# Head norm with its root on GpSimd and one VectorE step a head, and four changes of order, in a hybrid decoder step on one core

## The chip, the cores and the metric

The program runs on one core of one Trainium2 chip. A core has five engines, each with its own queue of instructions, which it works off in order: TensorE (PE in the profile; its weight loads are shown as PEld), VectorE (DVE), ScalarE (ACT), GpSimd (POOL) and SyncE (SP), which here only issues transfers. An instruction starts when the one ahead of it in its queue is done with issuing and the semaphores that it waits for have been raised. Data lies in SBUF, matmul results in the eight banks of PSUM, inputs and outputs in HBM. The metric is the time of one execution in device microseconds; a time quoted for a kernel is the median of several runs.

## What is computed

One inference step of a one-layer decoder on 544 tokens: a prompt of 512 tokens and 8 samples of 4 tokens each, D = 1024.

```python
proj = jnp.einsum('btd,de->bte', x, w_in) + b_in
q, k, v, g, ca, cg = jnp.split(proj, 6, axis=-1)
...
o, r_new = retention(q, k, v, r0, log_gamma)
ret_out = jax.nn.silu(g) * head_norm(o).reshape(b, t, RET_WIDTH)
conv_out, buf_new = conformer_conv(ca, cg, buf, dw_kernel, dw_bias, conv_ln_g, conv_ln_b)
mix = jnp.einsum('bte,ed->btd', jnp.concatenate([ret_out, conv_out], axis=-1), w_out)
x = layer_norm(ALPHA * x + mix, ln1_g, ln1_b)
ffn = peer(x.reshape(b * t, D_MODEL), w_query, sub_keys_1, sub_keys_2, peer_u, peer_v)
x = layer_norm(ALPHA * x + ffn.reshape(b, t, D_MODEL), ln2_g, ln2_b)
```

`head_norm` normalises each of the four heads' 128 outputs of a token: `(x - mean) * rsqrt(var + 1e-5)`. `peer` takes for each token and each of 8 heads the best 16 of 128 x 128 experts (the sum of two key scores), weighs each expert's output vector by a softmax gate times the gelu of the token's product with the expert's input vector, and adds them up.

## The kernel before

**Tokens and stages.** The first 128 prompt tokens, with the 32 sample tokens, go through projection, convolution, retention, output projection and norm first. Then come the other 384 prompt tokens, whose work shares the engines with the expert stage of the first 128. The experts are done in two ways. For the first 128 prompt tokens, the samples and the next 128 prompt tokens ("I", "Is" and "Ib" in the profile) GpSimd fetches each chosen expert's two vectors by an indirect transfer of 1 MB for 128 tokens (L587, line 587). VectorE takes the product (L590), ScalarE the gelu and the gate (L598, L599), and VectorE adds the weighted vector (L604). For the last 256 prompt tokens all experts are computed densely: for each of the 128 values of the first key ("rows" below) TensorE multiplies the 128 experts' input vectors with the tokens (`scores_of`, L815, weights from `ut`), ScalarE takes the gelu, the gates are spread into the same layout by a second kind of matmul (`build`: L893 to L906, multiplied in at L945, stored at L947 and L963), and TensorE multiplies the row's weights with its output vectors (`v_products`, L930, one load `v_row` of 512 KB each) into four PSUM banks, pB00 and pB01 for the first 128 of these tokens (b = 0), pB10 and pB11 for the others (b = 1).

**What sets the order.** The program is written in the order in which it is to be thought of. A scheduler with a model of durations then puts each engine's instructions into the order of their planned starts, the earlier written first where several are ready. `behind(a, b)` tells it to place `a` after `b`; it is a matter of order only and makes no semaphore. `hold` and `fence` use it to place gather products behind certain steps. Tiles come from pools that turn over a few buffers, so the next user of a buffer waits for the last reader of the one before: `mm` banks of PSUM (`mmps`; four in the key search), two score tiles in SBUF for `retrieve`, four buffers `uvp` for the rows, two PSUM tiles `sp` for a pair of rows' scores.

**Head norm** (`head_norm`, L317 to L336) is called five times: for chunk 0 of the prompt (L672), for the samples in `retain_s`, and for chunks 1 to 3 in `retain`. The retention output comes without the decay factor exp((i+1) log gamma) of its rows, so the norm multiplies the variance by the factor's square (`gq2`), adds epsilon and takes the root on GpSimd (`rsqrt`, L182 to L185), multiplies by the factor (`gq`), and makes a bias of minus mean times scale (L331, `hnb`); ScalarE then applies scale and bias to each head (L334, `on`). TensorE transposes the heads (`gate_heads`, L341) and VectorE multiplies them with the gates (L342).

**The other places.** Four loads of the samples' convolution cache `u_s` stand at L658 on GpSimd's queue, before the first gated projection. The chosen lists are turned into key sums for the build at L836 to L857, for g = 0 and 1: three transposes each (L848), behind the retrievals of all eight heads and ahead of those for "b" and "s" (`topk_of`, `retrieve` with scores L532, copies L535). While the first keys are built, `first_keys` multiplies the first eight rows for b = 0 alone (`AHEAD` = 8). `phases` then does b = 1 for rows 4 to 7, whose buffers still hold them, loads rows 0 to 3 a second time for b = 1, and goes on with row 8, both halves at once. The last four rows are loaded, and then written as all of b = 0 before all of b = 1; the two closing norms follow (L1021 on). The scheduler put these last sixteen products in the order of the rows, both halves of each in turn. `rope` (L201 on) copies a projected head to SBUF on ScalarE (L219), and TensorE then turns it (L209).

Of the kernel before, what the change touches and what calls it, by code (L numbers as in the profile page):

```python
# [24 lines left out]
CW, CK = 512, 31  # L25
# [19 lines left out]
def _consts():  # L45

    f = np.float32
    parts = {}
    pos = np.concatenate([np.arange(128), PAST + np.tile(np.arange(SQ), SB), np.arange(128, NP)]).astype(f)
    inv = (f(10000.0) ** (-np.arange(0, DH, 2, dtype=f) / f(DH))).astype(f)  # L50
    ang = (pos[None, :] * inv[:, None]).astype(f)
    cos, sin = np.cos(ang).astype(f), np.sin(ang).astype(f)
    parts["cos"] = np.concatenate([cos, cos], 0)
    parts["sin"] = np.concatenate([-sin, sin], 0)
    lg = np.log(1.0 - 2.0 ** (-5.0 - np.arange(H)))
    i = np.arange(C)
    mp = (i[:, None] <= i[None, :])[:, None, :] * (DH ** -0.5) * np.exp(-(i + 1.0)[:, None] * lg)[:, :, None]
    parts["mask_p"] = mp.reshape(128, -1)
    s = np.arange(NS)
    si, sb = s % SQ, s // SQ  # L60
    ms = ((sb[:, None] == sb[None, :]) & (si[:, None] <= si[None, :]))[:, None, :] * (DH ** -0.5)
    ms = ms * np.exp(-(si + 1.0)[:, None] * lg)[:, :, None]
    z = np.zeros((128, H * NS))
    z[:NS] = ms.reshape(NS, -1)
    parts["mask_s"] = z
    parts["kc_p"] = (DH ** -0.5) * np.exp((C - 1.0 - i)[:, None] * lg)
    parts["gq_p"] = np.exp((i + 1.0)[:, None] * lg)
    parts["gq2_p"] = np.exp(2 * (i + 1.0)[:, None] * lg)
    for n, v in (("kc_s", (DH ** -0.5) * np.exp((SQ - 1.0 - si)[:, None] * lg)),
                 ("gq_s", np.exp((si + 1.0)[:, None] * lg)), ("gq2_s", np.exp(2 * (si + 1.0)[:, None] * lg)),  # L70
                 ("blk", (sb[:, None] == np.arange(SB)[None, :]) * 1.0)):
# [23 lines left out]
def tile_step(ctx: ExitStack, tc: tile.TileContext, a, o):  # L95
# [222 lines left out]

    def head_norm(po, n, kind):

        st = small("hst", [128, H, 6])
        mv = small("hmv", [128, H, 2])
        for h in range(H):
            V.bn_stats(st[:n, h], po[:n, h * DH:(h + 1) * DH])
            V.bn_aggr(mv[:n, h], st[:n, h])
        rs = small("hrs", [128, H])
        V.tensor_mul(rs[:n], mv[:n, :, 1], cc("gq2_" + kind)[:n])
        rsqrt(rs[:n], rs[:n])
        V.tensor_mul(rs[:n], rs[:n], cc("gq_" + kind)[:n])
        nb = small("hnb", [128, H])  # L330
        steps[kind] = V.scalar_tensor_tensor(nb[:n], mv[:n, :, 0], -1.0, rs[:n], op0=OP.mult, op1=OP.mult)  # L331
        on = small("on", [128, 512])
        for h in range(H):
            S.activation(on[:n, h * DH:(h + 1) * DH], po[:n, h * DH:(h + 1) * DH], AF.Identity,  # L334
                         bias=nb[:n, h:h + 1], scale=rs[:n, h:h + 1])
        return on  # L336

    def gate_heads(on, n, gT, c0):
# [295 lines left out]
    for g, (w_, r_) in GSP.items():  # L634
# [19 lines left out]
    nc.sync.dma_start(cst[0], a["consts"])  # L654
    W0[2] = load_w(a["w_in"], 2 * 512, [t.rearrange("p (k e) -> p k e", k=8) for t in (
        gx.tile([128, 2 * D], F32, name="g"), per.tile([128, 8 * n], F32, name="x1T")[:, 0:2 * D])])
    for m in range(4):
        nc.gpsimd.dma_start(u_s[:, m, :, 0:CK - 1], a["cacheT"][m * 128:(m + 1) * 128])  # L658
    glu(W0[5], W0[4], xT0, 160, 0, 128)
    conv(y0, 128, 0)  # L660
    nc.scalar.dma_start(cst[1], a["consts2"])
    w = W0[2]
    v0 = project_v(w, xT0, 0, 128, lead2[:, 1280:1792])
    lastq = rope(load_win(0), 0, xT0, 160, 0, both(q0, qS))
    lastk = rope(load_win(1), 1, xT0, 160, 0, both(k0, kS))
    silu_gate(load_win(3), xT0, 160, both(g0, gS), True)
    normed = conv_norm(y0, 128)
# [135 lines left out]
    def place2(e):  # L803

        g = max(i for i in range(4) if E0S[i] <= e)
        return GW[g][:, e - E0S[g]:e - E0S[g] + 2]

    def scores_of(e, ne=1):

        sp = pdn.tile([128, 2, ND], F32, name="sp")  # L810
        for i in range(ne):
            u = uvp.tile([128, D], F32, name="uv").rearrange("p (k e) -> p k e", k=8)
            nc.sync.dma_start(u, a["ut"][e + i])
            for k in range(8):
                T.matmul(sp[:, i], u[:, k], x1T[:, k, NG2:], start=(k == 0), stop=(k == 7), skip_group_check=True)  # L815
        return sp[:, 0:ne] if ne > 1 else sp[:, 0]

    qs = rp.tile([128, 16, n], F32, name="qs")
# [14 lines left out]
            c0 = NG2 + 128 * g  # L833
            retrieve(lambda h, s: qs[:, h * 2 + s, c0:c0 + 128], [h0, h0 + 1], 128, 1, eg[:, g], eg[:, 2 + g], h0)
    wps.close()
    for g in range(2):  # L836
        ef = eg[:, g].rearrange("p h k -> p (h k)")
        ei = rp.tile([128, 128], I32, name="ei")
        V.tensor_copy(ei, ef)
        V.tensor_scalar(ei, ei, NK - 1, None, op0=OP.bitwise_and)  # L840
        e1 = rp.tile([128, 128], F32, name="e1")
        V.tensor_copy(e1, ei)
        e2 = rp.tile([128, 128], F32, name="e2")
        V.tensor_sub(e2, ef, e1)
        V.tensor_scalar(e2, e2, 1.0 / NK, None, op0=OP.mult)
        p = mmps().rearrange("p (q t) -> p q t", q=4)
        for q, t in enumerate((e1, e2, eg[:, 2 + g].rearrange("p h k -> p (h k)"))):
            T.transpose(p[:, q], t, ident)  # L848
        gr = rp.tile([128, 128], F32, name="e2")
        S.activation(gr, p[:, 2], AF.Copy)  # L850
        cs = slice(g * 128, (g + 1) * 128)
        S.activation(e1T[:, cs], p[:, 0], AF.Copy, scale=-1.0)
        S.activation(e2T[:, cs], p[:, 1], AF.Copy)
        for q in range(3):
            V.tensor_copy(gtT[:, q, cs], gr)
            if q < 2:
                V.tensor_sub(gr, gr, gtT[:, q, cs])  # L857
    topk_of("b", NS, range(0, PH, 2))
    topk_of("s", 0, range(2))
    for e in range(E0S[2], E0S[3], 2):  # L860
        S.activation(place2(e), scores_of(e, 2), AF.Gelu)
    gbs = ExitStack()
    gb = gbs.enter_context(tc.tile_pool(name="gb", bufs=1, side="right", reuse_waits="tile"))
    GW[0] = gb.tile([128, EG[0], ND], F32, name="Gb")
# [104 lines left out]
            v_products(e, vt, b)  # L969

    def phases():
        for e in [*range(AHEAD - UV, AHEAD), *range(AHEAD - UV)]:
            v_products(e, ahead[e] if e >= AHEAD - UV else v_row(e), 1)
            yield
        for e in range(len(ahead), EG[0]):
            v_stage(e)
            yield
        gbs.close()
        gd = ctx.enter_context(tc.tile_pool(name="gd", bufs=1, side="right", reuse_waits="tile"))
# [14 lines left out]
        ends = [(e, v_row(e)) for e in range(NK - UV, NK)]  # L994
        for b in range(2):
            for e, vt in ends:
                v_products(e, vt, b)
                yield

    def fetched():  # L1000
# [73 lines left out]
```

## Time and profile before

| | |
|---|---|
| timed runs, us | 1555.4, 1565.19, 1567.76; median 1565.19 |
| profiled execution, us | 1557.44, its span 1555.7 |
| mean granted TensorE clock over the span | 0.983 |
| VectorE, ScalarE, GpSimd busy, share of the span | 79%, 37%, 24% |
| bytes moved by transfers | 505.85 MB, mean 325 GB/s |
| share of the chain that ended last: PE, DVE, DMA, issue | 55%, 20%, 12%, 9% |

A line of a group or timeline names the source line, the engine and the operation, then the tile written and the tiles read, and the shapes. In a timeline the first number is the start in us from the beginning of the span and the second the duration, and a bracket at the end gives the engine's idle time before it and what ended that. Line numbers are those of the kernel before; in the changed kernel the same lines stand up to four lines earlier as far as the key search, and up to twelve later behind it.

### The profile page before, as it was taken

The numbers are of one execution on the slowest core, as the hardware profiler recorded it, in microseconds if no ns is written. First come the engines' busy times: TensorE is split into PE (matmuls) and PEld (weight loads), VectorE is DVE, ScalarE is ACT, GpSimd is POOL, SyncE is SP. The second block draws the span as 40 slices with busy tenths as digits, with TensorE's granted clock in tenths as the row PEclk, the third lists the DMA queues.
The fourth block names the chain that finished last, engine by engine and source line by source line (L and its number), as shares of the span: only waits on it lengthen the run. The fifth ranks groups of instructions, "written<-read, shape, count | busy, mean of one in ns | idle before, by whom it ended". The sixth has DMA issues, their size and how long they took to land.

```text
span 1555.7 us, 20736 instructions
## 1 busy us (share of the span) xinstructions
PE 1484.1 (95%) x7046; PEld 1004.1 (65%) x7046; DVE 1227.7 (79%) x3151; ACT 581.4 (37%) x1633; POOL 369.6 (24%) x329
## 2 busy tenths in 40 slices
PE   6999999897999999999999999999999999999997
PEld 6978667565866668788888884444566555543333
DVE  4779998978747999999978988666777777766664
ACT  2224453125112333333534898426992111111110
POOL 2001225322312222312231101222223222322210
PEclk9999999998999999999999999999999999999999
DMA  9648787985688779999999624999999999999993
GB/s 362 243 153 353 252 297 257 347 334 206 226 339 341 273 260 363 358 330 346 366 382 360 240 88 177 394 350 402 347 372 394 423 424 424 424 424 424 424 410 121
DMA packets 100119, 505.85 MB, mean 325 GB/s; under 512 B 10247, under 2 KB 21255, under 8 KB 57125
## 3 DMA queue, kind: packets, MB, share of 16 engines
q0 software_dynamic: 42240, 305.12, 50.4%
q1 hardware_dynamic: 51325, 192.05, 32.4%
q10 hardware_dynamic: 6448, 7.36, 1.5%
q8 instruction: 55, 0.90, 0.2%
q14 instruction: 51, 0.42, 0.1%
HBM read 499.12 MB, written 5.80 MB: 325 GB/s over the span
## 4 chain that ended last, share of the span: by engine, by line
PE 55%; DVE 20%; DMA 12%; issue 9%; POOL 3%; ACT 2%; DVEq 0%; SPq 0%; POOLq 0%; ACTq 0%
PE pB L930 27%; PE sp L815 11%; DMA g<-in_uv_dram,I 6%; PE mm L199 5%; PE mm L486 5%; DVE acc L604 4%; DVE g L590 4%; PE mm L906 3%; POOL g L587 2%; DMA g<-in_uv_dram,Is 2%; DMA g<-in_w_in_dram 2%; DMA uv<-in_uv_dram 1%; PE mm L310 1%; DVE B L901 1%; DVE score L516 1%
## 5 line engine op out<-in xcount | busy, mean ns | idle before, releaser
L815 PE MATMUL sp<-x1T,uv 128*128 128x256 f32 x2048 | 464.1, 383 | 5.2 <-DMA uv<-in_ut_dram 2.8
L604 DVE SCALAR_TENSOR_TENSOR acc<-g,wgt,acc 128x1024 f32<-128x1024 f32 x285 | 364.5, 1279 | 102.0 <-ACT wgt L599 100.4
L815 PEld LDWEIGHTS sp<-x1T,uv 128*128 128x128 f32 x2048 | 384.7, 191 | 78.5 <-issue 28.2
L598 ACT ACTIVATE act<-act 128x1 f32<-128x1 f32 x288 | 57.8, 201 | 625.7 <-DVE g L590 625.4
L587 POOL DMA_INDIRECT g<-in_uv_dram,I x128 | 166.9, 1304 | 460.1 <-DVE acc L604 259.2
L590 DVE SCALAR_TENSOR_TENSOR g<-g,x1g 128x1024 f32<-128x1024 f32 x160 | 195.2, 1222 | 71.8 <-DMA g<-in_uv_dram,Ib 50.5
L587 POOL DMA_INDIRECT g<-in_uv_dram,Ib x128 | 140.6, 1098 | 442.0 <-DVE acc L604 293.7
L199 PE MATMUL mm<-x1T,w 128*128 128x384 f32 (+1 forms) x512 | 178.3, 504 | 1.5 <-ACT score L535 1.2
L590 DVE SCALAR_TENSOR_TENSOR g<-g,x 128x1024 f32<-128x1024 f32 x128 | 154.8, 1214 | 31.0 <-DMA g<-in_uv_dram,I 30.9
L930 PE MATMUL pB<-uv,Ga 128*128 128x512 f32 x352 | 162.1, 604 | 0.2
L893 ACT ACTIVATE off<-row,e1T 128x128 bf16<-128x128 bf16 x512 | 158.0, 388 | 1.0
L199 PEld LDWEIGHTS mm<-x1T,w 128*128 128x128 f32 x512 | 97.4, 192 | 73.7 <-issue 40.3
L930 PE MATMUL pB<-uv,Gb 128*128 128x512 f32 x256 | 113.5, 597 | 4.9 <-DMA uv<-in_uv_dram 4.5
L930 PEld LDWEIGHTS pB<-uv,Ga 128*128 128x128 f32 x352 | 63.7, 189 | 83.4 <-issue 63.1
L930 PE MATMUL pB<-uv,Gd 128*128 128x512 f32 x256 | 115.5, 599 | 0.8
L930 PEld LDWEIGHTS pB<-uv,Gd 128*128 128x128 f32 x256 | 46.7, 190 | 69.7 <-issue 69.5
L930 PEld LDWEIGHTS pB<-uv,Gb 128*128 128x128 f32 x256 | 47.4, 190 | 60.7 <-issue 52.9
L906 PEld LDWEIGHTS <-A 128*128 128x128 bf16 x1536 | 60.5, 96 | 31.3 <-issue 21.3
L901 DVE TENSOR_TENSOR B<-M,gtT 128x768 bf16<-128x768 bf16 (+1 forms) x192 | 69.4, 416 | 9.4 <-PE mm L906 9.2
L930 PE MATMUL pB<-uv,Gc 128*128 128x512 f32 x160 | 72.8, 600 | 0.0
L895 ACT ACTIVATE A<-off 128x1024 bf16<-128x1024 bf16 x64 | 67.4, 1053 | 9.3 <-PE mm L906 8.5
L906 PE MATMUL mm<-B,A 128*128 128x96 bf16 (+1 forms) x1536 | 63.9, 191 | 7.3 <-DVE Gc L947 6.5
(274 smaller groups left out, 1675.4 us busy)
## 6 DMA issues: line engine op xcount, KB each, us to landing
uv<-in_uv_dram SPq DMA_DIRECT2D x132, 512.0 KB
uv<-in_ut_dram SPq DMA_DIRECT2D x128, 512.0 KB
w<-in_w_in_dram SPq DMA_DIRECT2D x18, 1024.0 KB
w<-in_w_query_dram SPq DMA_DIRECT2D x16, 1024.0 KB
w<-in_w_out_dram SPq DMA_DIRECT2D x7, 1024.0 KB
g<-in_uv_dram,I POOLq DMA_INDIRECT x128
keys<-in_state_retention_dram ACTq DMA_DIRECT2D x4, 512.0 KB
out_dram<-keys SPq DMA_DIRECT2D x4, 512.0 KB
```

Source lines behind the costliest of these rows:

```text
L199: T.matmul(p[:, :n], w[m // 2][:, k, (m % 2) * 128:(m % 2 + 1) * 128], xT[:, k, c0:c0 + n], start=(k == 0), stop=(k == 7))
L486: last = T.matmul(banks_[q][:n, s * 256:(s + 1) * 256], src[:, k, c0:c0 + n], wo[q * 2 + s][:, k0 + k, :], start=(xT is None and k0 == 4 a ...
L587: G.indirect_dma_start(out=t, out_offset=None, in_=a["uv"], in_offset=bass.IndirectOffsetOnAxis(ap=idx[:, k:k + 1], axis=0))
L590: dot = V.scalar_tensor_tensor(t[:, :D], t[:, :D], 1.0, x1, op0=OP.mult, op1=OP.mult, accum_out=act[:, 0:1])
L598: S.activation(act[:, 1:2], act[:, 0:1], AF.Gelu)
L604: V.scalar_tensor_tensor(acc, v, wgt, acc, op0=OP.mult, op1=OP.add)
L815: T.matmul(sp[:, i], u[:, k], x1T[:, k, NG2:], start=(k == 0), stop=(k == 7), skip_group_check=True)
L893: S.activation(off[:, t], row, AF.Abs, bias=e1T[:, t1 + t:t1 + t + 1])
L895: S.activation(A, off, AF.Relu, bias=1.0, scale=-1.0)
L901: V.tensor_tensor(B[:, q], M, pairs_of(gtT[:, q], t1).to_broadcast([128, TB // 2, ne, 2]), op=OP.mult)
L906: mm = T.matmul(pt[:, t % nt], A[:, t - t1], B[:, q, (t - t1) // 2, :, t % 2], start=(q == 0), stop=(q == 2))
L930: ps_.append(T.matmul(pB[b][q], W[:, b * 128:(b + 1) * 128], vt[:, q * 512:(q + 1) * 512], start=False, stop=(e == NK - 1), skip_group_che ...
```

## The change

Five edits. The head norm's decay factor moves into the constant: `ce` is epsilon divided by the factor's square, which is added to the variance, and the factor cancels, so `gq`, `gq2` and three small VectorE steps go. The add and the power run on GpSimd, and VectorE subtracts the mean and scales in one step a head, instead of ScalarE. The cache's four loads are written behind the first rotary projection, with `behind`. The key sums move into a function that is called after 34 of the 44 rows of a stretch have been written, and their transposes are placed behind the last matmul of the pair of rows just written. In `phases` the reloaded rows 0 to 3 alternate with rows 8 to 11. The last rows' b = 1 products are placed behind the last one of b = 0.

```diff
-    parts["gq_p"] = np.exp((i + 1.0)[:, None] * lg)
-    parts["gq2_p"] = np.exp(2 * (i + 1.0)[:, None] * lg)
+    parts["ce_p"] = EPS * np.exp(-2 * (i + 1.0)[:, None] * lg)
...
     def head_norm(po, n, kind):
...
         rs = small("hrs", [128, H])
-        V.tensor_mul(rs[:n], mv[:n, :, 1], cc("gq2_" + kind)[:n])
-        rsqrt(rs[:n], rs[:n])
-        V.tensor_mul(rs[:n], rs[:n], cc("gq_" + kind)[:n])
-        nb = small("hnb", [128, H])
-        steps[kind] = V.scalar_tensor_tensor(nb[:n], mv[:n, :, 0], -1.0, rs[:n], op0=OP.mult, op1=OP.mult)
+        G.tensor_add(rs[:n], mv[:n, :, 1], cc("ce_" + kind)[:n])
+        G.tensor_tensor(rs[:n], rs[:n], mhalf[:n].to_broadcast([n, H]), op=OP.pow)
         on = small("on", [128, 512])
         for h in range(H):
-            S.activation(on[:n, h * DH:(h + 1) * DH], po[:n, h * DH:(h + 1) * DH], AF.Identity,
-                         bias=nb[:n, h:h + 1], scale=rs[:n, h:h + 1])
+            steps[kind] = V.tensor_scalar(on[:n, h * DH:(h + 1) * DH], po[:n, h * DH:(h + 1) * DH], mv[:n, h, 0:1],
+                                          rs[:n, h:h + 1], op0=OP.subtract, op1=OP.mult)
...
-    for m in range(4):
-        nc.gpsimd.dma_start(u_s[:, m, :, 0:CK - 1], a["cacheT"][m * 128:(m + 1) * 128])
     glu(W0[5], W0[4], xT0, 160, 0, 128)
...
     lastq = rope(load_win(0), 0, xT0, 160, 0, both(q0, qS))
+    for m in range(4):
+        behind(nc.gpsimd.dma_start(u_s[:, m, :, 0:CK - 1], a["cacheT"][m * 128:(m + 1) * 128]), lastq)
...
             for k in range(8):
-                T.matmul(sp[:, i], u[:, k], x1T[:, k, NG2:], start=(k == 0), stop=(k == 7), skip_group_check=True)
+                latest[:] = [T.matmul(sp[:, i], u[:, k], x1T[:, k, NG2:], start=(k == 0), stop=(k == 7),
+                                      skip_group_check=True)]
...
-    for g in range(2):
+    def lists(g, mark):
...
         for q, t in enumerate((e1, e2, eg[:, 2 + g].rearrange("p h k -> p (h k)"))):
-            T.transpose(p[:, q], t, ident)
+            behind(T.transpose(p[:, q], t, ident), mark)
...
     for e in range(E0S[2], E0S[3], 2):
         S.activation(place2(e), scores_of(e, 2), AF.Gelu)
+        if e - E0S[2] == 32:
+            for g in range(2):
+                lists(g, latest[0])
...
     def phases():
-        for e in [*range(AHEAD - UV, AHEAD), *range(AHEAD - UV)]:
-            v_products(e, ahead[e] if e >= AHEAD - UV else v_row(e), 1)
+        for e in range(AHEAD - UV, AHEAD):
+            v_products(e, ahead[e], 1)
             yield
-        for e in range(len(ahead), EG[0]):
+        for e in range(AHEAD, EG[0]):
             v_stage(e)
+            if e < 2 * AHEAD - UV:
+                v_products(e - AHEAD, v_row(e - AHEAD), 1)
             yield
...
         for b in range(2):
             for e, vt in ends:
-                v_products(e, vt, b)
+                ps_ = v_products(e, vt, b)
+                if b:
+                    for p in ps_:
+                        behind(p, last)
+                else:
+                    last = ps_[-1]
                 yield
```

More of the change, by code (lines that the diff above doesn't have):

```diff
@@ L66, in _consts @@
     parts["kc_p"] = (DH ** -0.5) * np.exp((C - 1.0 - i)[:, None] * lg)
-    parts["gq_p"] = np.exp((i + 1.0)[:, None] * lg)
-    parts["gq2_p"] = np.exp(2 * (i + 1.0)[:, None] * lg)
+    parts["ce_p"] = EPS * np.exp(-2 * (i + 1.0)[:, None] * lg)
     for n, v in (("kc_s", (DH ** -0.5) * np.exp((SQ - 1.0 - si)[:, None] * lg)),
-                 ("gq_s", np.exp((si + 1.0)[:, None] * lg)), ("gq2_s", np.exp(2 * (si + 1.0)[:, None] * lg)),
+                 ("ce_s", EPS * np.exp(-2 * (si + 1.0)[:, None] * lg)),
                  ("blk", (sb[:, None] == np.arange(SB)[None, :]) * 1.0)):
@@ L806, in place2 @@
         return GW[g][:, e - E0S[g]:e - E0S[g] + 2]
+    latest = []
     def scores_of(e, ne=1):
```

## The prediction

> **What bounds the kernel now.** I read the page first, for which engine is full.
>
> ```profile
> span 1555.7 us, 20736 instructions
> ...
> PE 1484.1 (95%) x7046; PEld 1004.1 (65%) x7046; DVE 1227.7 (79%) x3151; ACT 581.4 (37%) x1633; POOL 369.6 (24%) x329
> ...
> L815 PE MATMUL sp<-x1T,uv 128*128 128x256 f32 x2048 | 464.1, 383 | 5.2 <-DMA uv<-in_ut_dram 2.8
> ```
>
> TensorE is busy in 1484.1 of 1555.7 us, idle in 71.6. The change removes no matmul, so it can gain only what TensorE waits for, what it loses at a lower clock, and the tail after its last matmul. One row of keys is 16 instructions of the L815 group, 16 x 464.1/2048 = 3.6 us; I use this unit below. The second view is the list of TensorE's waits (line waiting, what it waited for: us in total, times, longest).
>
> ```profile
> PE mm L341 <- ACT on L334: 9.6, 2, 6.6
> ...
> PE mm L906 <- DVE Gc L947: 6.5, 8, 1.7
> PE pB L930 <- DMA uv<-in_uv_dram: 4.5, 4, 1.8
> PE mm L209 <- ACT blk L219: 4.2, 1, 4.2
> PE mm L848 <- DVE e L842: 3.0, 1, 3.0
> ...
> PE mm L486 <- DVE g L342: 0.8, 1, 0.8
> ...
> PE mm L848 <- DVE e L845: 0.7, 1, 0.7
> ```
>
> Five of these belong to the change: the head norm (L341, 9.6, and its gate L342, 0.8), the key sums' transposes (L848, 3.7), the rows loaded again (L930, 4.5), and, through the order of ScalarE's queue, the rotary turn (L209, 4.2). The third view is the busy time by stretch: the first number is the stretch, then PE, PEld, DVE, ACT, POOL, and the granted clock, DMA share and GB/s last.
>
> ```profile
> 280.00:320.00 40.00, 35.76 (x105) 20.57 (x104) 39.87 (x62) 8.01 (x26) 14.55 (x12) 0.91 0.93 346
> 360.00:400.00 40.00, 31.70 (x154) 21.61 (x155) 31.39 (x63) 14.77 (x36) 15.79 (x15) 0.83 0.72 257
> 478.00:772.00 294.00, 284.56 (x1273) 226.16 (x1272) 286.43 (x1094) 99.30 (x240) 71.20 (x59) 0.99 0.89 327
> 836.00:958.00 122.00, 116.08 (x1060) 95.57 (x1057) 114.70 (x397) 109.04 (x312) 7.37 (x7) 0.99 0.50 178
> ```
>
> Two things stand here. Where TensorE waits long, its clock also falls: 0.83 over 360 to 400, against 1.00 or 0.99 in undisturbed stretches. And the key search (478 to 772) is full on both sides: TensorE 284.6, VectorE 286.4 of 294. A wait that goes there on one side may come back on the other.
>
> **Head norm.** For the prompt's chunks 2 and 3 the chain of events is this.
>
> ```profile
> 361.04 0.75 PE L341 MATMUL mm<-cst,on 128*128 128x128 f32 x4 [2.96 <-ACT on L334]
> 362.40 2.08 PE L357 MATMUL mm<-blk 128*128 128x128 f32 x8 [0.60 <-DVE Rst L381]
> 371.13 0.48 PE L341 MATMUL mm<-cst,on 128*128 128x128 f32 x1 [6.65 <-ACT on L334]
> ...
> 361.47 0.88 DVE L381 SCALAR_TENSOR_TENSOR Rst<-Rst,mm 128x128 f32<-128x128 f32 x4
> 362.26 0.37 DVE L325 BATCH_NORM_AGGREGATE hmv<-hst 128x2 f32<-128x6 f32 x4
> 363.10 0.62 DVE L253 SCALAR_TENSOR_TENSOR blk<-mm,cols,sg 128x384 f32<-128x384 f32 x1 [0.47 <-ACT sg L251]
> 363.63 1.28 DVE L604 SCALAR_TENSOR_TENSOR acc<-g,wgt,acc 128x1024 f32<-128x1024 f32 x1
> ...
> 364.90 0.68 DVE L359 TENSOR_TENSOR sc<-mm,cst 128x512 f32<-128x512 f32 x1
> ...
> 370.42 0.16 DVE L331 SCALAR_TENSOR_TENSOR hnb<-hmv,hrs 128x4 f32<-128x4 f32 x1
> ...
> 370.62 1.50 ACT L334 ACTIVATE on<-mm,hnb,hrs 128x128 f32<-128x128 f32 x4 [3.82 <-DVE hnb L331]
> ...
> 366.17 0.25 POOL L184 TENSOR_SCALAR hrs<-hrs 128x4 f32<-128x4 f32 x1
> 366.50 1.05 POOL L185 TENSOR_TENSOR hrs<-hrs,mhalf 128x4 f32<-128x4 f32 x1
> ```
>
> Before, a head norm is VectorE, GpSimd twice, VectorE twice (0.16 each), then four ScalarE steps (1.50). After, it is GpSimd's add and power, then four VectorE steps. The new step is not in this trace; its nearest row is the four L381 steps of the same 128x128 size, 0.88 us, and its upper end ScalarE's 1.50. The GpSimd add lies between the 0.25 of L184 and the 1.05 of L185; I take 0.25. VectorE so gains 20 x 0.22 = 4.4 us of work over five head norms and loses 15 small steps of 0.16 (2.4), on an engine that is not full here (31.4 of 40).
>
> In the changed program's queues (the built program's order, not a run) the four steps of the first chunk stand ahead of three gather products that L331 stood behind, so its transpose finds them done. For the second chunk they stand right after L359, and I walk VectorE's queue: L381 ends at 362.35 now, 0.9 later with the four new steps before it, 363.25; then the aggregates 0.37, two gather sums of 1.28 and two gate steps of 0.62, and L359's 0.68, in all 368.1; the first step ends at 368.3. TensorE takes its transpose there instead of at 371.13: **2.8 us**. It doesn't get the whole 9.6, because the score matmuls L357 between the two transposes wait for L381, which moves 0.9 us the other way: the 2.96 is mostly exchanged for a longer wait there. Bounds: 0 and 9.6. For chunk 1 the four steps start where L331 ended, so the 0.8 of L342 goes: **0.8 us**. GpSimd's queue puts the roots among the gathers at nearly the same places; behind a root wait only gathers whose buffers come free later anyway. The samples' norm hides under TensorE's conv and projections.
>
> The Trainium skill ("GPSIMD Engine Reference", section 4.1 Engine selection) advises against GpSimd for a two-input elementwise step, about twice as slow as VectorE. By that the add would cost about 2 x 0.16 = 0.3 instead of 0.25 and the sum would stay. No run here shows it yet.
>
> **The rotary turn.** This is an effect of queue order only.
>
> ```profile
> 290.87 0.20 ACT L598 ACTIVATE act<-act 128x1 f32<-128x1 f32 x1 [2.14 <-DVE g L590]
> ...
> 294.21 0.20 ACT L598 ACTIVATE act<-act 128x1 f32<-128x1 f32 x1 [2.81 <-DVE g L590]
> 294.45 0.30 ACT L599 ACTIVATE wgt<-act,GT 128x1 f32<-128x1 f32 x1
> 294.65 0.56 ACT L219 ACTIVATE blk<-mm,cols 128x384 f32<-128x384 f32 x1
> ...
> 295.26 1.65 PE L209 MATMUL mm<-blk,cst 128*128 128x384 f32 x2 [4.24 <-ACT blk L219]
> ```
>
> The copy L219 stands in ScalarE's queue behind a gather's activation, which waits for VectorE. In the changed order one pair of L598 and L599 fewer stands ahead of this copy. Behind the pair of 290.87 it would start 0.44 later, as it does now behind 294.21, and 0.9 later again for the four new VectorE steps: 292.2 instead of 294.65. So the wait shrinks by **2.4 us** (bounds 0 and 4.2).
>
> **Key sums' transposes.** They are put behind a matmul of row 33, and the scores of the next search (L532) move up in their place. The 3.7 us of L848 go. But what paces the stretch is VectorE, whose instructions before the first build step are the same but for one sum (L604). In the changed queue TensorE has 58 rows ahead of the first build product instead of 61, 3 x 3.6 = 10.8 us less to fill the time with. Those rows aren't lost: they come in the build, where TensorE waits 6.5 us for L947 and ScalarE is full 109 of 122. VectorE begins its search 12 L815 instructions (2.7 us) earlier and has up to 294 - 286.4 = 7.6 us of idle time to win. So the end of this stretch lies between 3.7 + 2.7 = 6.4 us of gain and 10.8 - 2.7 = 8.1 us of loss; I take **0**.
>
> **Late rows.** TensorE waits 4.5 us for four reloaded rows that need only half a row's matmuls each.
>
> ```profile
> 967.00 1.98 PE L930 MATMUL pB<-uv,Gb 128*128 128x512 f32 x4 [1.80 <-DMA uv<-in_uv_dram]
> ...
> 979.21 3.70 PE L930 MATMUL pB<-uv,Gb 128*128 128x512 f32 x8 [1.08 <-DMA uv<-in_uv_dram]
> ```
>
> Rows land about (979.21 - 967.00)/4 = 3.1 us apart. Half a row takes 1.8 us, so TensorE starves; a whole and a half row take 5.4 us for two loads, 2.7 each, so it starves less but later. The first 1.80 remains, since the first load comes no sooner. Of 2.7 I take **1.5 us** (bounds 0 and 2.7; SP's queue holds the same loads, in another order).
>
> **Last keys by halves.** The four banks end one after the other:
>
> ```profile
> 1489.36 57.03 PE L930 MATMUL pB<-uv,Gd 128*128 128x512 f32 x128
> ...
> 1543.85 0.70 DVE L452 BATCH_NORM_STATS2 lst<-pB 128x6 f32<-128x512 f32 x1 [18.17 <-PE pB L930]
> ...
> 1547.56 0.68 DVE L452 BATCH_NORM_STATS2 lst<-pB 128x6 f32<-128x512 f32 x1
> 1548.16 1.40 DVE L466 SCALAR_TENSOR_TENSOR g<-g,lrs,lnb 128x512 f32<-128x512 f32 x2
> ...
> 1551.22 1.41 DVE L466 SCALAR_TENSOR_TENSOR g<-g,lrs,lnb 128x512 f32<-128x512 f32 x2
> ```
>
> TensorE ends at 1546.39, but the last bank's statistics wait for the other half's norm until 1547.56, and its aggregate for that half's L466 until 1549.56. With one half done before the other's last eight matmuls, the first norm fits in VectorE's idle 18.17 us. The last bank then starts at about 1546.4, 1.1 us sooner, and the aggregate doesn't wait for L466 (1549.56 - 1547.56 - 0.68 = 1.3): **2.2 us** (bounds 1.1 and 2.4).
>
> **Cache loaded late: nothing.** In the changed program's GpSimd queue the four loads stand where they stood, after the memset and ahead of the norm's rows, with no wait. The order asked for binds only instructions of the same queue. I take 0.
>
> The sum is 2.8 + 0.8 + 2.4 + 0 + 1.5 + 2.2 = **9.7 us**. The profiled execution took 1557.44 us around its span of 1555.7; the three timed runs lie at 1555.4, 1565.19 and 1567.76, median 1565.19. The profiled one is 7.8 below the median, among the quick ones. I set the sum against the middle of both, 1561.3: 1551.6, or **1552 us**.
>
> The clock is not in the sum. At 0.83 over 40 us some 2 x 0.17 x 40 = 13.6 us ran at half speed, at 0.91 some 7.2; at most 6.8 and 3.6 us were lost. The Trainium skill ("TensorE: Matmul & The Clock Gate", section HAM oscillation) says that an idle gap of more than about 3.4 us halves the clock. The trace agrees in that the two stretches hold waits of 6.65 and 4.24. By that rule the turn's wait, cut to 1.8, would keep the full clock, and the sum would be up to 3.6 us larger; the head norm's new gap of some 4 us would still trip it.
>
> **Rivals.** (a) *The waits go entirely, and the clock with them.* 9.6 + 0.8 + 4.2 + 3.7 + 2.7 + 2.4 = 23.4 us, and up to 10.4 of clock: 1527 to 1538. For it speaks that the new steps depend on little; against it that L357 still waits for L381. Chance 0.20. (b) *The key search gives it back.* TensorE reaches the first build product before VectorE does and waits out its 8.1 us: 1561.3 - 9.7 + 8.1 = 1560. Chance 0.15. (c) *Slower: the search's scores stall TensorE in its queue.* L532 now stands among rows 8 to 30, each group needing a bank that a ScalarE copy frees, whose own target waits for a full VectorE; all L815 rows queue behind it. The price is the lost filler without recovery, 10.8, plus the ten later copies waiting 2 us each, 20: 30.8 - 9.7 gives 1582. It decides where VectorE runs more than a bank's turn behind the planned order. Against it: today's tight place there, L848, shows VectorE only 3.0 us late. Chance 0.12. (d) The forecast, from 1545 (the search's 6.4 won) to 1557 (half of its 8.1 lost): 0.53.
>
> **How the numbers follow.** A move of 1% (15.7 us from the median) is about what a measurement of this kernel can tell from none. Faster than 1549.5: all of (a) and about a third of (d), since 1552 lies just above: 0.37. Slower than 1580.8: two thirds of (c), 0.08. Within: 0.55. The range takes in (b), half of (a) and the 12 us spread of the runs: 1536 to 1566.
>
> **What would show it.** Right: L341's wait under 7 us, L209's under 2, L848 gone, the last statistics within 1.2 us of the last matmul, the cache loads issued as early as before. Wrong: new TensorE waits on L535's or L901's results between 560 and 780, or a first build product no earlier while the build ends later.

## The result, and the profile after

The changed kernel is slower: its ratio to the kernel before is 1.0037, 95% interval 1.0021 to 1.0053 (medians 1566.5 and 1560.82 us of 22 runs each), that is 5.8 us more (3.3 to 8.3). The forecast was 9.7 us less. So 15.5 us have to be found.

Single executions of one kernel differ by more than that: those of the kernel before lie between 1548.25 and 1571.91 us. A trace shows where things happen; what an edit costs is taken from timed ratios. The microseconds below are (ratio - 1) times the median of the kernel before in the same series.

The page of the changed kernel:

```profile
span 1563.2 us, 20740 instructions
...
PE 1485.9 (95%) x7046; PEld 1004.7 (64%) x7046; DVE 1233.6 (79%) x3156; ACT 575.1 (37%) x1613; POOL 369.9 (24%) x329
```

TensorE is busy 1.8 us longer and idle 5.7 us longer. Its waits are listed here for the changed kernel (line waiting, what it waited for: us in total, times, longest). L338 is the old L341, L354 the old L357, L529 and L532 the search's scores and their copies, L911 the build's product.

```profile
PE mm L529 <- ACT score L532: 7.3, 5, 3.0
...
PE mm L294 <- ACT sg L293: 5.1, 3, 4.4
PE mm L354 <- DVE Rst L378: 4.6, 1, 4.6
PE mm L338 <- DVE on L331: 3.9, 1, 3.9
PE mm L529 <- DMA keys<-in_keysT_dram: 3.3, 1, 3.3
PE mm L354 <- DVE blk L212: 2.6, 2, 2.5
PE pB L935 <- DMA uv<-in_uv_dram: 2.5, 2, 1.9
PE mm L911 <- DVE B L906: 2.4, 3, 1.8
...
PE sp L814 <- ACT Gb L871: 2.0, 1, 2.0
...
PE mm L208 <- ACT blk L218: 1.0, 1, 1.0
```

Every wait that the prediction named is shorter: the head norm's 9.6 is 3.9, the turn's 4.2 is 1.0, the key sums' 3.7 is gone, the reloaded rows' 4.5 is 2.5. (The turn's wait is not as firm a figure as it looks; see below.) But new ones stand in the list: 7.3 and 3.3 us at the search's scores, 4.4 at the sums of the convolution's norm (L294), 4.6 before L354, and 2.0 and 2.4 around the first build product.

Two of the stretches shown before (PE, PEld, DVE, ACT, POOL, granted clock, DMA share, GB/s):

```profile
280.00:320.00 40.00, 36.54 (x116) 21.07 (x115) 38.84 (x61) 8.16 (x27) 12.26 (x11) 1.00 0.93 363
...
478.00:772.00 294.00, 284.47 (x1253) 225.83 (x1253) 282.22 (x1087) 98.69 (x236) 69.19 (x57) 0.98 0.88 320
```

From 478 to 772 TensorE is as busy as before (284.5 us) but gets through 1253 instructions instead of 1273; the rest is left for later. VectorE, which had 286.4 of 294, now has 282.2.

To see where the two executions part, take the time at which TensorE has done the same amount of work (its matmuls added up at their quick rate). The table gives how much longer each stage of the kernel before (by its times) took in four other traces. The kernel with the tail's edits alone has the queue order of the kernel before up to 934 us, so its column shows what chance does; the last two columns belong to experiments below.

| stage of before, us | changed | tail's edits alone | edits, old search order | no edits, new search order |
|---|---|---|---|---|
| 0 to 108 | -1.4 | -2.5 | -2.3 | -2.0 |
| 108 to 349 (turn) | +1.9 | +3.2 | +1.3 | +5.2 |
| 349 to 404 (head norm) | -2.4 | -0.1 | -2.1 | +0.8 |
| 404 to 468 | 0.0 | 0.0 | +1.3 | +1.3 |
| 468 to 772 (search) | +10.8 | +3.7 | +0.8 | +14.8 |
| 772 to 888 (build) | -2.5 | +5.1 | +4.2 | +1.1 |
| 888 to 1003 (reloaded rows) | +3.0 | -2.4 | -2.3 | +0.3 |
| 1003 to last matmul | +0.3 | +0.9 | +2.8 | +0.8 |
| after the last matmul | -2.3 | -2.3 | -2.2 | 0.0 |

Two rows are steady: the head norm's stage and the end. The rest swings by 3 to 5 us with no edit at all. The search stands out. (The last column is of an execution of 1579.81 us, 8.5 above the median of its kernel, so its 14.8 is not that kernel's usual loss.)

The search's 10.8 us have two parts. TensorE's waits between 474 and 780 us add up to 15.0 us, where the kernel before has 9.4: 5.6 more. And its clock falls in three places of the changed kernel's search, where it falls in one of the kernel before; the first three rows are the changed kernel's, the last is the kernel before's:

```profile
474.00:484.00 10.00, 6.82 (x26) 6.28 (x27) 6.67 (x24) 2.25 (x7) 0.94 (x1) 0.66 1.01 419
...
578.00:583.00 5.00, 4.79 (x16) 4.00 (x17) 4.65 (x19) 2.23 (x6) 1.00 (x1) 0.66 0.68 234
...
667.00:672.00 5.00, 4.05 (x26) 3.18 (x27) 5.00 (x27) 1.26 (x4) 1.92 (x2) 0.66 0.92 344
```

```profile
648.00:652.00 4.00, 3.89 (x11) 3.21 (x12) 2.63 (x6) 2.44 (x3) 1.44 (x1) 0.57 0.87 314
```

By the granted clock 0.34 x 20 = 6.8 us are lost in the one and 0.43 x 4 = 1.7 in the other: 5.1 more. The two parts make 10.7. So about half of what the search lost in this trace went at the lower clock behind the waits.

### The profile page after: what moved, and what is told of

Its sections match the earlier page's. It is cut to its first block, busy times and chain, and to the rows that moved or that the text cites. A ratio compares the mean times of both kernels' runs of the same rounds, so it can differ in the third digit from the quotient of the medians.

```text
span 1563.2 us, 20740 instructions
## 1 busy us (share of the span) xinstructions
PE 1485.9 (95%) x7046; PEld 1004.7 (64%) x7046; DVE 1233.6 (79%) x3156; ACT 575.1 (37%) x1613; POOL 369.9 (24%) x329
## 4 chain that ended last, share of the span: by engine, by line
PE 55%; DVE 16%; DMA 12%; ACT 8%; issue 5%; POOL 2%; SPq 0%; DVEq 0%; POOLq 0%; ACTq 0%
PE pB L935 23%; PE sp L814 14%; PE mm L198 8%; DMA g<-in_uv_dram,I 6%; PE mm L483 4%; ACT off L898 4%; DVE acc L601 4%; DVE g L587 3%; POOL g L584 2%; ACT A L900 2%; DMA g<-in_w_in_dram 2%; PE mm L911 2%; DMA uv<-in_ut_dram 1%; DMA out_dram<-on 1%; PE mm L263 1%
## 5 line engine op out<-in xcount | busy, mean ns | idle before, releaser
L814 PE MATMUL sp<-x1T,uv 128*128 128x256 f32 x2048 | 466.0, 384 | 7.2 <-DMA uv<-in_ut_dram 2.4
L814 PEld LDWEIGHTS sp<-x1T,uv 128*128 128x128 f32 x2048 | 386.3, 192 | 81.2 <-issue 21.4
L911 PEld LDWEIGHTS <-A 128*128 128x128 bf16 x1536 | 60.2, 96 | 35.7 <-issue 20.6
L911 PE MATMUL mm<-B,A 128*128 128x96 bf16 (+1 forms) x1536 | 64.3, 191 | 10.6 <-DVE Gc L952 6.4
L906 DVE TENSOR_TENSOR B<-M,gtT 128x768 bf16<-128x768 bf16 (+1 forms) x192 | 69.3, 417 | 5.1 <-PE mm L911 5.1
```

The lines of the kernel that those rows point to most:

```text
L814: latest[:] = [T.matmul(sp[:, i], u[:, k], x1T[:, k, NG2:], start=(k == 0), stop=(k == 7), skip_group_check=True)]
L906: V.tensor_tensor(B[:, q], M, pairs_of(gtT[:, q], t1).to_broadcast([128, TB // 2, ne, 2]), op=OP.mult)
L911: mm = T.matmul(pt[:, t % nt], A[:, t - t1], B[:, q, (t - t1) // 2, :, t % 2], start=(q == 0), stop=(q == 2))
```

## The experiments

All were timed in five rounds beside the kernel before, with 11 or 12 runs of each (6 of the kernel without edits in the new search order). An interval reaches some 2.5 to 4.5 us to either side, and that of a difference between two of these kernels somewhat further; where the ranges of two theories lie closer together than that, the text says into which the middle falls, and no more is shown. The first eight kernels take the change apart.

**One edit each.** Three kernels have the kernel before with one group of hunks of the change, and one has the changed kernel with one group left as it was:

```diff
...
+        G.tensor_add(rs[:n], mv[:n, :, 1], cc("ce_" + kind)[:n])
+        G.tensor_tensor(rs[:n], rs[:n], mhalf[:n].to_broadcast([n, H]), op=OP.pow)
...
```

is the first (with the constants and the step a head, as in the diff of the change),

```diff
...
+            behind(T.transpose(p[:, q], t, ident), mark)
...
+        if e - E0S[2] == 32:
+            for g in range(2):
+                lists(g, latest[0])
```

the second. The third has `phases` as changed, and the fourth every hunk of the change but those of the second.

> The kernel before with the new head norm alone (constant, root on GpSimd, one VectorE step a head). Theory A, queue order: the edit shortens the plan ahead of the key search, so TensorE's queue has 16 score matmuls between the last query projection and the first scores of the search, where the kernel before has 42. The 26 missing ones are 26 x 0.227 = 5.9 us; the kernel before reached this point about 1.3 us after the keys landed, so TensorE waits some 4.6 us for them, and some 3 us go at half clock behind it. The head norm itself gives 2 to 3 us, and the wait that leaves the rotary turn comes back at the matmuls behind it. Sum: 2 to 7 us slower than before. Theory B, the key sums' edit alone is to blame: 4 to 7 us faster than before, as forecast for these terms (2.8 + 0.8 + 2.4).

Measured 1.0047 (1.0018 to 1.0077), 7.3 us slower (2.8 to 12.0): theory A's sign, just above its range, and B is out for this edit. Its trace has the wait for the keys, at 16 score matmuls ahead of the search's first scores, where the kernel before has 42:

```profile
PE mm L529 <- DMA keys<-in_keysT_dram: 5.4, 1, 5.4
```

> The kernel before with the key sums' transposes moved alone. Theory A: 42 score matmuls stand ahead of the first scores of the search, so no wait for the keys; but the scores of the later searches wait for copies (some 3 us at 570 us, smaller ones at 600 to 670), and the first build product comes with 59 rows done instead of 61: 3 to 7 us slower than before. Theory B: the whole difference between what was forecast and what came lies here, 15 us slower than before.

Measured 1.0026 (1.0002 to 1.0049), 4.1 us slower: theory A's range, far from B's 15.

> The kernel before with the reloaded rows alternating and the last rows by halves, nothing else. Everything up to about 930 us as before. Both theories: the time between the last matmul and the end shrinks by 2.2 to 2.4 us; the reloaded rows give 0 to 2 us. Sum: 2 to 4 us faster. A rival, that the alternation only moves the wait for these rows: TensorE's waits for reloaded rows sum to 4.5 us as before, and the whole is 2.3 us faster.

Measured 0.9997 (0.9971 to 1.0022). The interval reaches from 4.5 us faster to 3.4 slower, so it holds the expected 2 to 4 but doesn't show them; the trace does for the end (below). The rival, that the wait for reloaded rows only moves, falls: 2.3 us in this trace; over the ten traces with this edit the waits lie between 2.2 and 4.5, 2.9 on the mean, over the six without it between 4.2 and 4.8.

> The changed kernel with the key sums where they were before. Theory A: 30 score matmuls stand ahead of the first scores of the search, as in the changed kernel, so the wait for the keys (3 us, and 3 more at half clock) stays; the later searches' waits for copies go; the last rows by halves stay. Sum: between 3 us faster and 3 us slower than before. Theory B: 9 to 10 us faster than before, the forecast.

Measured 1.0024 (1.0003 to 1.0044), 3.7 us slower. B is out: without the key sums' edit the other four don't gain 9.7 us, they lose. A's range is just missed, and the wait for the keys that A named wasn't there in the trace, since the keys happened to land in time. So two different edits, the head norm and the key sums, each cost 4 to 7 us, and each has 59 rows of scores ahead of the first build product (score matmuls in the trace by then, 16 a row), the changed kernel 58, the kernel before 61.

**Rows put ahead.** Is it these rows? The scores of four rows are written ahead of the search's first scores, which are placed behind the 21st of their 32 matmuls:

```diff
...
             S.activation(qs[:, h0 * 2 + m], project(w, m, x1T, 0, n), AF.Copy)
+        if h0 == 0:
+            for e in (E0S[2], E0S[2] + 2):
+                S.activation(place2(e), scores_of(e, 2), AF.Gelu)
...
+                    if mark is not None:
+                        behind(mm, mark)
```

> The changed kernel with the first four rows' scores written between the query projection and the search's first scores, which are placed behind 21 of their instructions. In TensorE's queue 64 score matmuls (14 us) now stand ahead of the first scores instead of 30, and 62 rows ahead of the first build product instead of 58. Theory C, rows ahead of the build: VectorE sets when the first product can be taken (its first M came at 771.6 to 776.1 us in six traces), so each row fewer in the queue ahead of it is 3.6 us of TensorE's time lost for good; then this kernel wins back most of 4 x 3.6 = 14 us in the build, pays 1 to 3 us for the later search, and comes out 4 to 10 us under the changed kernel: 1556 to 1562 us. Theory D, the waits for banks and copies inside the search: those stay, only the wait for the keys (3.3 us and some 3 us of half clock) goes: 2 to 6 us under the changed kernel, and the build (first to last product of the first keys) stays longer than 190 us.

Measured 1.0001 (0.9978 to 1.0024), level with the kernel before and 5.6 us under the changed kernel by the ratios: C's range, and the top of D's. The sign that D named beside it didn't come: the build took 179 us in this trace, where D asked for more than 190 (194 in the changed kernel's trace, 181 in that of the kernel before).

> The changed kernel with the first build product placed behind row 61 and nothing else; it lands behind 63 rows. Theory C says that rows ahead of the product count only as far as TensorE would otherwise be idle there: in the changed kernel it waited 2.0 us for its first product and 2.0 us for ScalarE at 748, so the product comes 5 x 3.6 - 2 to 4 = 14 to 16 us later, the build gets that much shorter, and the whole is 0 to 4 us under the changed kernel. A rival, that the rows in the build are what costs: 10 us under it.

```diff
...
+                    if t == 0 and q == 0 and e0 == 0:
+                        behind(mm, done_mm[487])
```

Measured 1.0037 (1.0015 to 1.0060), as the changed kernel. The rival falls: rows in the build don't cost by being there.

> The changed kernel with the key sums where they were before, and the four rows written ahead of the first scores: 64 score matmuls ahead of them, 61 rows ahead of the first build product, as many as in the kernel before. Theory C: with the row count restored, what the other edits give is seen: head norm 2.4, last rows by halves 2.3, reloaded rows 0 to 1.5, less 1 to 3 us for the later search: 1 to 5 us faster than before. Theory D: the waits that the head norm's edit brought into the search stay: 0 to 4 us slower than before.

Measured 1.0022 (1.0003 to 1.0041), 3.4 us slower: C missed, D held.

> The kernel before with the last rows by halves, the reloaded rows alternating, and the four rows written ahead of the first scores; 61 rows ahead of the first build product as before. It is the control of the filling edit: where rows were not missing it gives nothing, and the later first scores may cost 0 to 3 us. Theories C and D: between 4 us faster and 1 us slower than before, by the 3.8 us of the tail and the reloaded rows less that cost.

Measured 1.0038 (1.0012 to 1.0064), 5.9 us slower: both missed. A kernel with all its 61 rows ahead loses 6 us by the filling alone. So the count of rows explains two of these four results and not the others. But each of these plans also gives the three engines another order through the whole search.

**The order itself.** The next kernels hold queues in a given order, instruction by instruction, from 30 matmuls ahead of the search's first scores to the 48th build product, by recording what the kernel issues and chaining it; this places, and makes no wait:

```diff
+    for name, runs in PIN.items():
+        order = [MADE[name][r] for r0, count in runs for r in range(r0, r0 + count)]
+        for one, two in zip(order, order[1:]):
+            behind(two, one)
```

> The changed kernel with the key sums where they were before, and the queues of TensorE, VectorE and ScalarE held in the order of the kernel before, instruction by instruction, from 30 matmuls ahead of the search's first scores to the 48th build product. So head norm, cache, reloaded rows and last halves are as changed, and the search stands as before (42 score matmuls ahead of the first scores, 61 rows ahead of the first build product). Theory O, the loss lies in the order of the search that the plan made anew: without it the edits give 2.5 (head norm) + 2.3 (last halves) + 0 to 1.5 (reloaded rows) us: 3 to 7 us faster than before. Rival E, the edits themselves cost in the stages before the search: 0 to 7 us slower, as with the order left free.

Measured 0.9971 (0.9955 to 0.9988), 4.5 us faster: theory O. The version beats both kernels.

> The kernel before, with none of the edits, its three queues held through the search in the order that the plan made for the changed kernel with the key sums where they were before (30 score matmuls ahead of the first scores, 59 rows ahead of the first build product). Theory O: 4 to 10 us slower than before, 2 x 3.6 us for the two rows of it. Rival E: as before, within 2 us.

Measured 1.0063 (1.0038 to 1.0089), 9.8 us slower, with no edit in it: theory O again. The two add up to 5.3; with the order left free the same edits cost 3.7 (0.5 to 6.9), which agrees. Waits in the search of this kernel (474 to 780 us), TensorE's and then VectorE's:

```profile
PE sp L815 <- ACT Ga L861: 5.7, 4, 2.9
PE mm L199 <- ACT score L535: 5.0, 2, 2.7
PE mm L848 <- DVE e L842: 4.3, 1, 4.3
PE sp L815 <- DMA uv<-in_ut_dram: 1.8, 1, 1.8
```

```profile
DVE g L590 <- DMA g<-in_uv_dram,I: 17.8, 11, 6.6
```

The kernel before has 1.2 us for copies of scores there, 0.2 for Ga, and 9.5 for VectorE's wait on gathered vectors. In this trace the new order makes TensorE wait for ScalarE's copies and gelus, and VectorE for gathers.

> The changed kernel with its TensorE queue held through the search in its own order but for the score matmuls of the rows, which stand earlier: 42 traced ones ahead of the first scores instead of 30, and, the surplus growing evenly, 61 rows ahead of the first build product instead of 58. All five edits stay. Theory O (rows ahead): the 5.7 us to the kernel before come back and some of the 5 to 6 us of the other edits show: 4 to 10 us under the changed kernel. A rival, that the key sums' place costs by itself: 0 to 3 us under it.

Measured 1.0022 (1.0003 to 1.0041): 2.3 us under the changed kernel by the ratios. By the middle, theory O in the form that it has there, that rows moved ahead on TensorE do it alone, missed, and the rival's 0 to 3 us held; the intervals don't part the two.

> As the kernel with the old order of three queues, but with TensorE's alone held; VectorE and ScalarE are in the order that the plan chooses around it. If TensorE's order is what costs: 3 to 7 us faster than before. If it is the order on VectorE, on which the search's steps queue among the gathers' sums: 0 to 7 us slower, as with the order left free.

Measured 0.9997 (0.9977 to 1.0017), from 3.6 us faster to 2.7 slower: between the two, 4 us short of the kernel with all three queues held and 4 us better than the same edits with no queue held. By the middles TensorE's order brings back some of the loss, not all; the interval reaches into both ranges.

The last two split the 9.8 us, in the kernel before:

> The kernel before, with none of the edits; TensorE's queue stays as it is through the search (61 rows ahead of the first build product), VectorE's and ScalarE's are held in the order that cost 9.8 us together with TensorE's. If the rows ahead are what costs (theory C): 0 to 2 us slower than before. If it is the order in which VectorE takes the search's steps and the gathers' sums (theory V): 5 to 10 us slower, with more than 15 us of waits for gathered vectors between 474 and 780 us, where the kernel before has 9.5.

Measured 1.0050 (1.0029 to 1.0070), 7.8 us slower (4.5 to 10.9), with all 61 rows ahead: theory C is out as the whole account. Its trace has 14.4 us of waits for gathered vectors, just under the 15 that V asked for.

> The kernel before, with none of the edits; TensorE's queue alone held in the order of the changed kernel with the key sums where they were before (30 score matmuls ahead of the first scores, 59 rows ahead of the first build product), VectorE and ScalarE as the plan chooses around it. Theory C: 5 to 10 us slower than before. Theory V: 0 to 4 us slower, what is left of the 9.8 us.

Measured 1.0039 (1.0013 to 1.0064), 6.1 us slower (2.0 to 10.0): by the middle in C's range, but the interval reaches into V's too. What these two show is that VectorE's and ScalarE's new order costs time beside TensorE's old one, and that TensorE's new order costs time with the others planned around it. The middles add up to 13.9 us, more than the 9.8 of all three together, which speaks for a loss that belongs to the orders as a set and not to one queue; the intervals are too wide to show that.

## Why the prediction was wrong

**How the queues hang together.** One stall of the changed kernel shows it, in the timelines of TensorE, ScalarE and VectorE (start, duration, engine, what; idle time before it at the end):

```profile
578.21 0.73 PE L529 MATMUL mm<-keys,qs 128*128 128x128 f32 x4 [2.98 <-ACT score L532]
```

```profile
575.81 0.20 ACT L595 ACTIVATE act<-act 128x1 f32<-128x1 f32 x1 [6.62 <-DVE g L587]
576.04 0.29 ACT L596 ACTIVATE wgt<-act,GT 128x1 f32<-128x1 f32 x1
576.36 1.28 ACT L567 ACT_TABLE_LOAD   x1
577.65 0.23 ACT L567 ACTIVATE ex<-ex 128x32 f32<-128x32 f32 x1
577.79 0.37 ACT L532 ACTIVATE score<-mm 128x256 f32<-128x256 f32 x1
```

```profile
571.86 0.97 DVE L564 TENSOR_REDUCE eg<-pick 128x32 f32<-128x800 int16 x1
572.74 0.32 DVE L514 MAX8 sv<-cand 128x8 f32<-128x50 f32 x2
572.97 1.27 DVE L601 SCALAR_TENSOR_TENSOR acc<-g,wgt,acc 128x1024 f32<-128x1024 f32 x1
574.16 0.48 DVE L514 MAX8 vf<-score 128x8 f32<-128x128 f32 x2
574.55 1.22 DVE L587 SCALAR_TENSOR_TENSOR g<-g,x 128x1024 f32<-128x1024 f32 x1
```

TensorE wants a bank, which a copy of scores on ScalarE (577.79) has to empty. The copy stands behind a gather's activation (575.81), and ScalarE has idled 6.62 us for that one's product, which stands on VectorE behind search steps and a gather's sum and runs at 574.55. Nobody is short of work; each has its next thing behind something else's. About half of the 2.98 us is ScalarE's own work ahead of the copy, an exponential with its table load (576.36 and 577.65). The number of such loads isn't what differs between the kernels: all sixteen traces have 58, and 27 or 28 of them between 474 and 780 us. All L814 rows queue behind L529 meanwhile, and the clock falls after it (0.66 over 578 to 583).

Over all sixteen traces one pair of waits goes with the order. Between 474 and 780 us TensorE's waits for copies of scores and for the rows' gelus (Ga, Gb) add up to 1.4 to 2.1 us in the three kernels that have the old order on all three queues (the kernel before, the tail's edits alone, the edits with the search held), and to 5.0 to 10.7 us in the thirteen others. VectorE's waits for gathered vectors don't part them: 9.5 to 13.2 us in those three, 7.4 to 19.7 in the others, 9.9 in the changed kernel. That TensorE's waits for ScalarE are the cause of the loss is argued from this; no run changed them alone.

**The step that failed** is the one on the key sums' transposes. It bounded the search from -6.4 to +8.1 and took 0, on the ground that VectorE paces the stretch and its instructions before the first build step "are the same but for one sum". The same instructions in another order are not the same pace: in the kernel before, with no edit, an order that the planner made for four of the five edits cost 9.8 us (5.9 to 13.9). For the changed kernel's own search the figure is the step from the edits with the search held, 4.5 us faster, to the changed kernel, 5.8 slower: 10.3 us, the key sums' edit included. Two things went wrong in it. The order was read as unchanged because its members were, and it was charged to the key sums' edit alone, where the head norm's edit brings a like one (59 rows ahead, 16 score matmuls ahead of the keys). The bound of 8.1 us, worked out from the three rows, had the size of it; the value taken did not. Rival (c), TensorE's own stall behind the search's scores with 30.8 us of loss, had the place and the sign right (7.3 us on L529, the sign that the prediction said would show it wrong), and the price much too high. Rival (b) was not it: TensorE's longest wait for the first build's steps (L911 for L906) was 1.8 us, not 8.1.

All five signs that were to show the forecast right came (L341's wait 3.9 us, L209's 1.0, L848's gone, the last statistics at once, the cache loads as early), and the time went the other way. They looked at the edits' own places only.

**Head norm, 3.6 us: mechanism right, size 2.4.** Timeline of the changed kernel, chunks 2 and 3:

```profile
362.74 0.88 DVE L378 SCALAR_TENSOR_TENSOR Rst<-Rst,mm 128x128 f32<-128x128 f32 x4
...
363.67 2.05 PE L354 MATMUL mm<-blk 128*128 128x128 f32 x8 [4.56 <-DVE Rst L378]
...
364.52 1.14 POOL L327 TENSOR_TENSOR hrs<-hmv,cst 128x4 f32<-128x4 f32 x1 [0.82 <-DVE hmv L325]
...
365.73 1.03 POOL L328 TENSOR_TENSOR hrs<-hrs,mhalf 128x4 f32<-128x4 f32 x1
...
368.59 0.68 DVE L356 TENSOR_TENSOR sc<-mm,cst 128x512 f32<-128x512 f32 x1
...
369.19 1.36 DVE L331 TENSOR_SCALAR on<-mm,hmv,hrs 128x128 f32<-128x128 f32 x4
369.65 0.47 PE L338 MATMUL mm<-cst,on 128*128 128x128 f32 x1 [3.93 <-DVE on L331]
```

The queue stands as walked: the four steps are right behind L356, and the wait of 2.96 turned into one of 4.56 before L354. The four steps (now L331) took 1.36 us instead of 0.88, and the transpose came at 369.65 instead of 371.13, where 368.3 was forecast. Nine traces with this edit give 1.8 to 2.5 us less in this stage, seven without it (that of the kernel before, which counts as 0, is one of them) 0.6 less to 0.8 more; the means differ by 2.4.

**The rotary turn, 2.4 us: a wait of one execution.** L208 waits 1.0 instead of 4.2, and the clock over 280 to 320 is 1.00 instead of 0.91, which is what the Trainium skill's rule on idle gaps ("TensorE: Matmul & The Clock Gate", section HAM oscillation) would give. But this says little of the edit. The kernel with the tail's edits alone has the queue order of the kernel before here, and in its trace the same turn waits for nothing:

```profile
294.32 1.75 PE L209 MATMUL mm<-blk,cst 128*128 128x384 f32 x4
```

Of the seven traces without the head norm's edit three have this wait (4.2, 5.6 and 6.1 us) and four have none; of the nine with it six have 0.8 to 3.0 and three none. So the 4.2 us that the term was read from is in part chance. Nor is the stage from 108 to 349 us shorter: against the kernel before, nine traces with the head norm's edit have 2.4 us more there on the mean (0.6 less to 7.1 more), seven without it 0.4 more (3.7 less to 5.2 more). One wait in it did grow: L294, for a ScalarE step on VectorE's differences, takes 2.2 to 4.4 us of this stage in the nine traces with the edit, 0.9 to 2.1 in the seven without. VectorE is busy 38.84 of 40 here, 39.87 before; that it is the full engine which sends the time elsewhere is argued, not shown.

**Last keys by halves, 2.2 us: right.** The time after the last matmul:

```profile
1555.42 0.70 DVE L449 BATCH_NORM_STATS2 lst<-pB 128x6 f32<-128x512 f32 x1 [2.10 <-PE pB L935]
1556.28 0.70 DVE L449 BATCH_NORM_STATS2 lst<-pB 128x6 f32<-128x512 f32 x1 [0.16 <-PE pB L935]
...
1558.77 1.42 DVE L463 SCALAR_TENSOR_TENSOR g<-g,lrs,lnb 128x512 f32<-128x512 f32 x2
```

The last statistics start 0.04 us after the last matmul (1539.77 + 16.47 = 1556.24). From there to the end are 7.0 to 7.1 us in all ten traces with this edit, 9.3 in the six without.

**Late rows, 1.5 us: right** as far as the waits show it (4.5 to 2.9 on the mean, 1.6; in three of the ten traces they are still 3.6 to 4.5). **Cache, 0: right**: its loads are issued at 2.7 us in both kernels.

What the edits give where the search is held, 2.4 + 2.3 + 1.6 = 6.3 us, lies in the interval measured for that kernel (1.9 to 7.0). Of the 15.5 us between forecast and result some 10.3 fall to the search, 2.4 to the turn and 1.2 to the head norm; the other 1.6 are less than the intervals.

Two things stay open. Which of the many exchanged places cost most wasn't tried, so why the new order is worse is not shown. And neither the kernel before held in its own order nor the changed kernel with all five edits held in the old one was run.

## What to carry to other kernels

Where a planner orders the queues, an edit's price includes the new order of every stage behind it, and a stage in which two engines are full is the one to look at first: compare its order before and after, and count a difference there as a cost with a sign to be measured. Hold the order of that stage while testing an edit, and the edit's own worth appears; hold it for good, and it may be kept: here 4.5 us. Before a wait is priced, look for it in a second execution: the turn's 4.2 us were missing in one with the same queue order. And let the signs that are to show a forecast right include one at the stage behind the edit.

## What was not expected of the hardware

The granted clock fell after shorter gaps than the prediction reckoned with. In the changed kernel TensorE idled 3.25 us for the keys and 2.98 us at 578:

```profile
477.00:481.00 4.00, 3.82 (x17) 3.85 (x18) 1.80 (x5) 0.77 (x2) 0.67 (x1) 0.50 1.02 426
...
577.90:582.00 4.10, 3.79 (x12) 3.17 (x13) 3.65 (x15) 2.03 (x4) 0.56 (x1) 0.61 0.69 232
```

The Trainium skill ("TensorE: Matmul & The Clock Gate", section HAM oscillation) puts the limit at about 3.4 us; the rows show half speed after less. A gap of 2.46 us, which ended at 316.92 us, left the clock at 1.00 over 280 to 320.

On GpSimd the same addition of two 128x4 tiles takes very different times. In the changed kernel it took 0.20 us for chunks 0 and 1 of the prompt and 1.14 and 1.07 for chunks 2 and 3; over the nine traces with this edit it is about 0.2 in 18 of 36 cases, 1.07 to 1.14 in 12 and 2.20 in 6. The prediction estimated 0.25, and a VectorE step of that size takes 0.16. Half of the cases lie within the factor of about two that the Trainium skill ("GPSIMD Engine Reference", section 4.1 Engine selection) gives, the other half far above it; what decides between them wasn't tried. The 1.14 cost nothing, since VectorE was busy with other work until 369.2.
